# The prologue of a hybrid GLA and S5 block, put in another order

## The chip, the cores and the metric

The kernel runs on one core of one Trainium2 chip. The metric is the device time of one execution in microseconds (us), of which the median over several runs is taken; lower is better. The kernel before took 1011.63 us in the median of three runs (1009.40 to 1013.76).

## The reference, cut to what matters

One decoder block over 512 tokens, ahead of which 16 meta tokens are put. The model width is 1024. All numbers are float32.

```python
h = concatenate([meta, x])                       # 528 tokens x 1024
xn = rmsnorm(h, g_mix_pre)                       # x / sqrt(mean(x*x) + 1e-6) * gain
proj = xn @ w_in                                 # q, k, v, r, a_low, u, z_gla, z_ssm
log_a = log_sigmoid(a_low @ w_gate_up + b_gate) / 16
o = gla_chunked(q, k, v, log_a)                  # 4 heads, cumulative sums of log_a
...
# S5: 64 groups, 64 states, 16 channels each
lam = exp(a_re*dt) * (cos(a_im*dt), sin(a_im*dt))
bb = ((lam - 1) / a) * (b_re, b_im)              # (64, 64, 16), complex
y = Re(C scan(lam, bb u)) + d_skip * u
...
h = h + rmsnorm(mixed @ w_out, g_mix_post)       # gates, GLU and merge before it
h = h + rmsnorm(square(relu(hn @ w_ff1)) @ w_ff2, g_ffn_post)
```

## The kernel before

The program is written for a framework that takes the instructions in source order, gives each tile its memory, and sets the order in which each engine gets its instructions by a planner of its own when it is built. Source order is the priority; an instruction whose inputs the planner takes to be late can be passed by a later one. Each engine then runs its own list strictly in order, and so do the queues that issue loads (SP's, ScalarE's and GpSimd's). A tile in a memory pool that was opened after another was closed can lie on that one's memory, and its first writer then waits until the old tile is done with.

Every large product is done in three exact passes: a weight tile is split by `load_w` into a high part (ScalarE, line 101) and the remainder (VectorE, line 114), as are the activations (`transpose_tokens`, lines 101 and 138), and `mm3` (lines 121 to 123) adds high by high, high by low and low by high. `feat_tile` does this over the 8 tiles of the inner dimension, so a product of one weight tile of 128 columns with 264 tokens (half of the 528, `HALF`) is 24 matmuls. Raw weights and their two parts have three buffers each.

The part that is changed runs from the start to the first S5 block. In source order:

- **Constants.** A first activation on ScalarE at line 75 brings in its function table.
- **Input norm** (lines 166 to 206). Four tiles of 128 tokens are loaded by SP (line 178), the 16 meta tokens and the gain, broadcast to 128 partitions, by ScalarE's queue (lines 181 and 182). There are two groups: the meta tokens with tiles 0 and 1, then tiles 2 and 3. For each group come the sums of squares (line 195), the inverse root by an integer guess and three Newton steps on VectorE (`rsqrt`, 13 small instructions), the multiplication by root and gain (line 201) and the transposes on TensorE (line 135), with the split into `xh` and `xl`.
- **GLA gates** (lines 212 to 257). The 16 columns of `a_low` (48 matmuls of 16 columns), the product with `w_gate_up` (line 245), Abs, Exp and Ln on ScalarE (lines 247 to 250), and a scan on VectorE (line 255), written to DRAM as `bd`.
- **S5 parameters** (lines 260 to 444). Some 100 small instructions on VectorE give the powers of lambda (`Lr`, `Li`, `E8`). `c_re` and `c_im` come by GpSimd's queue (lines 411 and 412), and TensorE transposes them (line 417). `b_re` and `b_im` are loaded by SP in transposed order into `ra` and `rb`, two halves each (lines 423 to 426), in runs of 16 numbers; line 429 gives `rb` its sign. `BA` and `BB` follow from them (lines 434 to 440). Most of it depends on nothing but its own loads.
- **u products** (lines 454 to 462). Eight weight tiles, two halves of tokens each. ScalarE copies each half out of PSUM into `ut` (line 461), and GpSimd's queue writes that to DRAM as `ud`. The four PSUM banks named `mm` hold four halves. `ut` lies in pool `pgb`, which is opened after the gates' pool `pga` was closed.

After it four S5 blocks alternate with four GLA heads. An S5 block first forms its matrices on VectorE from `CA`, `CB`, `BA`, `BB` and the powers (lines 593 to 595), transposes one of them on TensorE (line 600) and later reads `ud`. A GLA head does four weight tiles of q, k and v (lines 470 to 520) and reads `bd`. Then come the gates' products, the merge, the output product and the MLP, which the change leaves alone.

Of the kernel before, what the change touches and what calls it, by code (L numbers as in the profile page):

```python
# [9 lines left out]
F32R = mybir.dt.float32r  # L10
# [6 lines left out]
P = 128  # L17
D = 1024
# [28 lines left out]
def hybrid_block(ctx: ExitStack, tc: tile.TileContext, io, out: bass.AP):  # L47
# [25 lines left out]
    warm = mk(cst, [P, 1], tag="warm")  # L73
    V.memset(warm, 1.0)
    S.activation(warm, warm, AF.Square)
# [27 lines left out]
    def load_w(src, ncol=256):  # L103
        """src: [K, ncol] in DRAM -> list of (hi, lo) [P, K/P, 128]."""
# [13 lines left out]
    def mm3(ps, whi, wlo, xhi, xlo, kt):  # L118
        """ps += w.T @ x by three exact passes; whi(k), xhi(k) give the k-th tiles."""
        for k in range(kt):  # L120
            PE.matmul(ps, whi(k), xhi(k), start=(k == 0), stop=False)  # L121
            PE.matmul(ps, whi(k), xlo(k), start=False, stop=False)  # L122
            PE.matmul(ps, wlo(k), xhi(k), start=False, stop=(k == kt - 1))  # L123

    def feat_tile(w, xh, xl, c0, c1, ps, m=P, kt=KT):
        hi, lo = w
        mm3(ps, lambda k: hi[:, k, :m], lambda k: lo[:, k, :m], lambda k: xh[:, k, c0:c1], lambda k: xl[:, k, c0:c1], kt)
# [12 lines left out]
    def cmul(pl, orr, oi, ar, ai, br, bi, shape, tag, eng=V, bufs=1):  # L140
        """o = a * b (complex), o apart from a and b"""
# [11 lines left out]
    def erot(E, n, m, pl):  # L153
        """E[:, :, :, n+1 : n+m+1] = E[..., n] * E[..., 1 : m+1], E [P, (re, im), g, c]"""
# [10 lines left out]
    # ================= input norm =================  # L165
# [5 lines left out]
    xl = mk(px, [P, KT, NT], F32R, tag="xl")  # L171
    sx = ExitStack()
    pxt = pool("pxt", stack=sx)
    gpre = mk(pxt, [P, D], tag="gpre")
    xts = []
    for t in range(TT):
        xt = mk(pxt, [P, D], tag="xt", bufs=5)
        nc.sync.dma_start(xt, io["x"][0, t * P : (t + 1) * P, :])
        xts.append((xt, P, NM + t * P))
    xm = mk(pxt, [P, D], tag="xt", bufs=5)  # L180
    nc.scalar.dma_start(xm[:NM], io["meta_tokens"])
    nc.scalar.dma_start(gpre, io["g_mix_pre"][0].partition_broadcast(P))
# [4 lines left out]
    xts = [(xm, NM, 0)] + xts  # L187
# [3 lines left out]
    for a, b in ((0, 3), (3, 5)):  # L191
        for i in range(a, b):
            xt, n, col = xts[i]
            sq = mk(pxt, [P, D], tag="xsq", bufs=2)
            S.activation(sq[:n], xt[:n], AF.Square, accum_out=ss[:n, i : i + 1])
        V.tensor_scalar(ss[:, a:b], ss[:, a:b], 1.0 / D, EPS, op0=ALU.mult, op1=ALU.add)
        rsqrt(rs[:, a:b], ss[:, a:b], pxt, f"xr{a}")
        for i in range(a, b):
            xt, n, col = xts[i]
            xn = mk(pxt, [P, D], tag="xn", bufs=2)  # L200
            V.scalar_tensor_tensor(xn[:n], xt[:n], rs[:n, i : i + 1], gpre[:n], op0=ALU.mult, op1=ALU.mult)
            transpose_tokens(xn[:n], n, xh, xl, col)
# [5 lines left out]
    w_in = io["w_in"][0]  # L208

    w_in = io["w_in"][0]  # L210

    # ================= GLA gates =================
    sg = ExitStack()
    pg = pool("pg", stack=sg)
# [15 lines left out]
    wgu = mk(pga, [16, 512], tag="wgu")  # L230
    nc.gpsimd.dma_start(wgu, io["w_gate_up"][0])
    wa = load_w(w_in[:, C_A : C_A + 16], 16)[0]
    alow = mk(pga, [16, NT], tag="alow")
    for i in range(2):
        ps = bank("mm")
        feat_tile(wa, xh, xl, i * HALF, (i + 1) * HALF, ps[:16, :HALF], m=16)
        S.copy(alow[:, i * HALF : (i + 1) * HALF], ps[:16, :HALF])
# [14 lines left out]
    for h in range(HEADS):  # L252
# [3 lines left out]
        nc.gpsimd.dma_start(bd[h], b2)  # L256
    sga.close()

    # ================= S5 parameters =================
# [8 lines left out]
    E8 = mk(p5, [P, 2, GRP, 9], tag="E8")  # L268
    V.tensor_reduce(i16, ident.rearrange("p (b h) -> p h b", h=HG), axis=mybir.AxisListType.X, op=ALU.add)
# [645 lines left out]
```

## Time and profile before

| what | value |
| --- | --- |
| median of three runs | 1011.63 us (1009.40 to 1013.76) |
| span of the profiled execution | 1011.4 us |
| TensorE busy, over the span | 954.4 us |
| VectorE busy | 573.3 us |
| ScalarE busy | 366.1 us |
| GpSimd busy | 61.3 us |

The profile gives no other time of that execution than its span, from the first to the last instruction. In its views a line names the start and the length in us, the engine, the line of the kernel, the operation and the tiles (out<-in). PE is TensorE, PEld its weight load, DVE is VectorE, ACT is ScalarE, POOL is GpSimd; SPq is the queue that issues SP's loads. A name of a tile without a number stands for all its buffers. The row of windows gives the busy time of each engine in a stretch, with the granted TensorE clock as a share of full speed. TensorE's matmuls overlap, so the time between their starts, not the duration of one, tells what a matmul costs.

### The profile page before, as it was taken

The numbers are of one execution on the slowest core, as the hardware profiler recorded it, in microseconds if no ns is written. First come the engines' busy times: TensorE is split into PE (matmuls) and PEld (weight loads), VectorE is DVE, ScalarE is ACT, GpSimd is POOL, SyncE is SP. The second block draws the span as 40 slices with busy tenths as digits, with TensorE's granted clock in tenths as the row PEclk, the third lists the DMA queues.
The fourth block names the chain that finished last, engine by engine and source line by source line (L and its number), as shares of the span: only waits on it lengthen the run. The fifth ranks groups of instructions, "written<-read, shape, count | busy, mean of one in ns | idle before, by whom it ended". The sixth has DMA issues, their size and how long they took to land.

```text
span 1011.4 us, 13388 instructions
## 1 busy us (share of the span) xinstructions
PE 954.4 (94%) x5120; PEld 806.1 (80%) x5120; DVE 573.3 (57%) x1098; ACT 366.1 (36%) x600; POOL 61.3 (6%) x128
## 2 busy tenths in 40 slices
PE   1779999999999999999999999899999999999996
PEld 1669978998878888888888877788888878888884
DVE  4979785968662787764544667633232343333327
ACT  3434344545443343333532432233222242332321
POOL 3110101010101101110000000000000000000000
PEclk9879999999999999999999999999999999999998
DMA  9534634252535564545854662042323254233202
GB/s 192 147 118 123 143 97 116 75 140 63 135 109 146 140 164 130 148 129 156 251 146 129 203 185 83 36 124 84 104 84 104 84 193 137 86 104 99 89 22 83
DMA packets 166080, 123.98 MB, mean 123 GB/s; under 512 B 33692, under 2 KB 148448, under 8 KB 166016
## 3 DMA queue, kind: packets, MB, share of 16 engines
q1 hardware_dynamic: 158944, 101.31, 36.2%
q0 software_dynamic: 6464, 19.65, 6.3%
q10 hardware_dynamic: 608, 2.16, 0.6%
q8 instruction: 40, 0.66, 0.3%
q14 instruction: 24, 0.20, 0.1%
HBM read 102.03 MB, written 16.81 MB: 117 GB/s over the span
## 4 chain that ended last, share of the span: by engine, by line
PE 78%; DVE 10%; issue 3%; DMA 3%; ACT 3%; SPq 2%; DVEq 0%; POOL 0%; ACTq 0%; POOLq 0%
PE mm L121 17%; PE mm L122 17%; PE mm L123 17%; PE mm L872 8%; PE sm L872 8%; PE sm L605 1%; PE sm L628 1%; PE sm L654 1%; PE sm L655 1%; SPq L424 1%; DVE wlo L114 1%; PE sm L600 1%; DMA wraw<-in_w_out_dram 1%; DMA vv<-vv 1%; DMA rb<-in_b_re_dram 1%
## 5 line engine op out<-in xcount | busy, mean ns | idle before, releaser
L114 DVE TENSOR_TENSOR wlo<-wraw,whi 128x1024 fp32r<-128x1024 f32 (+1 forms) x105 | 127.3, 1213 | 165.0 <-ACT whi L101 159.0
L101 ACT ACTIVATE whi<-wraw 128x1024 fp32r<-128x1024 f32 (+1 forms) x105 | 110.5, 1053 | 243.2 <-PE mm L122 217.0
L121 PE MATMUL mm<-xh,whi 128*128 128x264 f32 (+2 forms) x560 | 187.3, 335 | 6.3 <-ACT ut L461 4.5
L123 PE MATMUL mm<-xh,wlo 128*128 128x264 f32 (+2 forms) x560 | 186.4, 333 | 1.1 <-DVE wlo L114 1.1
L122 PE MATMUL mm<-xl,whi 128*128 128x264 f32 (+2 forms) x560 | 186.8, 334 | 0.0
L121 PEld LDWEIGHTS mm<-xh,whi 128*128 128x128 f32 (+1 forms) x560 | 104.7, 187 | 18.1 <-ACT ut L461 4.7
L123 PEld LDWEIGHTS mm<-xh,wlo 128*128 128x128 f32 (+1 forms) x560 | 104.8, 187 | 11.4 <-DVE wlo L114 1.3
L122 PEld LDWEIGHTS mm<-xl,whi 128*128 128x128 f32 (+1 forms) x560 | 104.8, 187 | 10.9 <-issue 1.0
L121 PE MATMUL mm<-hh,whi 128*128 128x512 f32 (+1 forms) x288 | 106.9, 372 | 0.0
L122 PE MATMUL mm<-hl,whi 128*128 128x512 f32 (+1 forms) x288 | 106.8, 371 | 0.0
L123 PE MATMUL mm<-hh,wlo 128*128 128x512 f32 (+1 forms) x288 | 106.6, 371 | 0.0
L863 DVE TENSOR_TENSOR fl<-f,fh 128x512 fp32r<-128x512 f32 x32 | 22.0, 692 | 84.6 <-ACT fh L101 84.6
L121 PEld LDWEIGHTS mm<-hh,whi 128*128 128x128 f32 x288 | 54.4, 190 | 10.4 <-ACT hh L101 0.2
L122 PEld LDWEIGHTS mm<-hl,whi 128*128 128x128 f32 x288 | 54.4, 189 | 10.3
L123 PEld LDWEIGHTS mm<-hh,wlo 128*128 128x128 f32 x288 | 54.3, 188 | 10.3
L101 ACT ACTIVATE fh<-f 128x512 fp32r<-128x512 f32 x32 | 20.0, 630 | 101.3 <-PE sm L872 101.3
L123 PE MATMUL mm<-gh,wlo 128*128 128x512 f32 x128 | 50.6, 395 | 0.0
L121 PE MATMUL mm<-gh,whi 128*128 128x512 f32 x128 | 50.6, 395 | 0.0
L122 PE MATMUL mm<-gl,whi 128*128 128x512 f32 x128 | 50.6, 395 | 0.0
L859 DVE TENSOR_TENSOR w2l<-wraw,w2h 128x1024 fp32r<-128x1024 f32 x32 | 39.1, 1225 | 7.2 <-ACT w2h L101 7.2
L872 PE MATMUL mm<-w2h,fh 128*128 128x512 f32 x128 | 40.0, 394 | 2.1 <-ACT fh L101 2.1
L872 PE MATMUL mm<-w2h,fl 128*128 128x512 f32 x128 | 40.3, 397 | 0.0
(378 smaller groups left out, 1655.7 us busy)
## 6 DMA issues: line engine op xcount, KB each, us to landing
wraw<-in_w_ff_dram SPq DMA_DIRECT2D x64, 512.0 KB, 4.0
wraw<-in_w_in_dram SPq DMA_DIRECT2D x48, 512.0 KB, 4.4
wraw<-in_w_glu_dram SPq DMA_DIRECT2D x16, 512.0 KB, 4.4
vv<-vv POOLq DMA_DIRECT2D x32, 130.0 KB, 3.3
xt<-in_x_dram SPq DMA_DIRECT2D x8, 512.0 KB, 5.6
M<-kpad SPq DMA_DIRECT2D x64, 64.0 KB, 3.4
wraw<-in_w_o_gla_dram SPq DMA_DIRECT2D x8, 512.0 KB, 4.4
wraw<-in_w_out_dram SPq DMA_DIRECT2D x8, 512.0 KB, 4.1
```

The source lines that it names most:

```text
L101: S.activation(dst, src, AF.Copy, scale=scale)
L114: V.tensor_sub(lo[:, :, :n], raw[:, :, :n], f32(hi)[:, :, :n])
L121: PE.matmul(ps, whi(k), xhi(k), start=(k == 0), stop=False)
L122: PE.matmul(ps, whi(k), xlo(k), start=False, stop=False)
L123: PE.matmul(ps, wlo(k), xhi(k), start=False, stop=(k == kt - 1))
L424: nc.sync.dma_start(ra[64:], bim)
L600: PE.transpose(ps[:, g * P : (g + 1) * P], MB[:, g0 + g].rearrange("p s h -> p (s h)"), ident)
L605: PE.matmul(ps[:, g * HG : (g + 1) * HG], M2[:, g, 0:8, :].rearrange("p l h -> p (l h)"), BA[:, blk * GB + g, :], start=True, stop=True)
L628: PE.matmul(pv[:, g], M1[:, g0 + g, :], U[:, g0 + g, :NST], start=True, stop=True)
L859: V.tensor_sub(lo, raw, f32(hi))
L863: V.tensor_sub(fl, f[:, k], f32(fh))
L872: PE.matmul(acc[t][n], a[:, ts_], b[:, n * 512 : (n + 1) * 512], start=st, stop=en)
```

## The change

The prologue is written in another order, and five things in it are done in another way.

- **Norm by tile.** Each token tile has its own root, but the meta tokens share that of tile 0. The root is a Sqrt activation on ScalarE, a reciprocal and one Newton step on VectorE. The table brought in at the start is the one with Sqrt. The gain comes as one row and is spread over 128 partitions by two products with a row of ones.
- **u first.** The first two weight tiles of u are loaded right behind x. The first token half of the first one is computed once the meta tokens and two tiles are there, that of the second behind the transposes of the third tile, and the two second halves follow behind the fourth. `ut` and `ud` move to pools that are opened before the norm.
- **Gates next, then the other six u tiles, then the S5 parameters.** The high and low parts of the 16 gate columns are put side by side in one weight tile of 32 columns, so 32 matmuls replace 48; `w_gate_up` is loaded twice, one copy under the other, and adds the two parts up. The gate columns' tile no longer uses the weights' buffers but pool `pga`, which lies on the norm's memory.
- **Held.** `tc.issue_after(i)` puts what is written inside it behind instruction i in the list of i's engine. The S5 parameters' work on VectorE stands behind the norm's last multiplication, and their loads on SP behind the last load of x.
- **b and c.** b is loaded as it lies (three loads, 64 partitions) and transposed by TensorE, 32 transposes in four PSUM tiles, with the sign given on the way out. c is loaded by SP's queue in place of GpSimd's.

```diff
-    S.activation(warm, warm, AF.Square)
+    S.activation(warm, warm, AF.Sqrt)
...
+    def root(y, ssum, pl, tag):
...
+        S.activation(a, ssum, AF.Sqrt, scale=1.0 / D, bias=epst[: shape[0]])
+        V.tensor_scalar(hm, ssum, 0.5 / D, 0.5 * EPS, op0=ALU.mult, op1=ALU.add)
+        V.reciprocal(y, a)
+        V.tensor_mul(a, y, y)
+        V.tensor_mul(a, a, hm)
+        V.tensor_scalar(a, a, -1.0, 1.5, op0=ALU.mult, op1=ALU.add)
+        return V.tensor_mul(y, y, a)
...
+    def u_half(w, ut, q):
+        ps = bank("mm")
+        last = feat_tile(w, xh, xl, q * HALF, (q + 1) * HALF, ps[:, :HALF])
+        S.copy(ut[:, :, q * 33 : (q + 1) * 33].rearrange("p s c -> p c s"), ps[:, :HALF].rearrange("p (c s) -> p c s", s=T8))
+        return last
...
+    def u_tile(shape=[P, T8, NCK]):
+        return mk(pg, shape, tag="ut", bufs=2)
...
+    nc.scalar.dma_start(grow, io["g_mix_pre"][0].rearrange("(o d) -> o d", o=1))
...
-    nc.scalar.dma_start(gpre, io["g_mix_pre"][0].partition_broadcast(P))
...
+    for i in range(2):
+        ps = bank()
+        PE.matmul(ps, one_row, grow[:, i * 512 : (i + 1) * 512], start=True, stop=True)
+        S.copy(gpre[:, i * 512 : (i + 1) * 512], ps)
...
-    for a, b in ((0, 3), (3, 5)):
-        for i in range(a, b):
...
-        V.tensor_scalar(ss[:, a:b], ss[:, a:b], 1.0 / D, EPS, op0=ALU.mult, op1=ALU.add)
-        rsqrt(rs[:, a:b], ss[:, a:b], pxt, f"xr{a}")
...
+    for i, (xt, n, col) in enumerate(xts):
+        sq = mk(pxt, [P, D], tag="xsq", bufs=2)
+        squared = S.activation(sq[:n], xt[:n], AF.Square, accum_out=ss[:n, i : i + 1])
+        if i == 0:
+            continue
+        a = 0 if i == 1 else i
+        root(rs[:, a : i + 1], ss[:, a : i + 1], pxt, f"xr{min(i, 2)}")
+        for xt, n, col in xts[a : i + 1]:
...
+            normed = V.scalar_tensor_tensor(xn[:n], xt[:n], rs[:n, j : j + 1], gpre[:n], op0=ALU.mult, op1=ALU.mult)
+            with ExitStack() as after:
+                if i > 2:
+                    after.enter_context(tc.issue_after(fed.ins))
+                transpose_tokens(xn[:n], n, xh, xl, col)
+        if i == 2:
+            with tc.issue_after(loaded.ins), tc.issue_after(squared.ins), tc.issue_after(normed.ins):
+                uw = load_w(w_in[:, C_U : C_U + 256])
+            uts = [u_tile() for _ in uw]
+        if i in (2, 3):
+            fed = u_half(uw[i - 2], uts[i - 2], 0)
+    for i in range(2):
+        u_half(uw[i], uts[i], 1)
+        u_out(i, uts[i])
...
-    wa = load_w(w_in[:, C_A : C_A + 16], 16)[0]
...
+    wraw = mk(pga, [P, KT, 16], tag="waraw")
+    nc.sync.dma_start(wraw, w_in[:, C_A : C_A + 16].rearrange("(k p) n -> p k n", p=P))
+    wa = mk(pga, [P, KT, 32], F32R, tag="wa")
...
+        for k in range(KT):
+            PE.matmul(ps[:32, :HALF], wa[:, k, :], xh[:, k, sl], start=(k == 0), stop=False, skip_group_check=True)
+            PE.matmul(ps[:16, :HALF], wa[:, k, :16], xl[:, k, sl], start=False, stop=(k == KT - 1), skip_group_check=True)
...
+    for c in range(256, D, 256):
+        for i, w in enumerate(load_w(w_in[:, C_U + c : C_U + c + 256])):
...
+    held = ExitStack()
+    held.enter_context(tc.issue_after(normed.ins))
+    held.enter_context(tc.issue_after(loaded.ins))
...
-        nc.gpsimd.dma_start(cnat[:, :, i, :], src)
-        nc.gpsimd.dma_start(cnatx[:, :, 1 - i, :], src)
+        nc.sync.dma_start(cnat[:, :, i, :], src)
+        nc.sync.dma_start(cnatx[:, :, 1 - i, :], src)
...
-    bre, bim = (io[n][0].rearrange("g n h -> n g h") for n in ("b_re", "b_im"))
-    nc.sync.dma_start(ra[:64], bre)
-    nc.sync.dma_start(ra[64:], bim)
-    nc.sync.dma_start(rb[:64], bim)
-    nc.sync.dma_start(rb[64:], bre)
+    bn = mk(q5, [N, 3, N, HG], tag="bn")
+    for i, name in enumerate(("b_re", "b_im", "b_re")):
+        nc.sync.dma_start(bn[:, i], io[name][0])
...
-    V.tensor_scalar_mul(rb, rb, nsgn)
+    for i, dst in enumerate((ra, rb)):
+        for h0 in range(0, HG, 8):
+            ps = bank()
+            pv = ps.rearrange("p (h g) -> p h g", h=8)
+            for h in range(8):
+                PE.transpose(pv[:, h], bn[:, i : i + 2, :, h0 + h], ident[:N, :N])
+            d = dst[:, :, h0 : h0 + 8].rearrange("p g h -> p h g")
...
-    for c in range(0, D, 256):
-        for i, w in enumerate(load_w(w_in[:, C_U + c : C_U + c + 256])):
-            blk = c // P + i
-            ut = mk(pgb, [P, T8, NCK], tag="ut", bufs=2)
...
```

More of the change, by code (lines that the diff above doesn't have):

```diff
@@ L74, in hybrid_block @@
     V.memset(warm, 1.0)
-    S.activation(warm, warm, AF.Square)
+    S.activation(warm, warm, AF.Sqrt)
+    epst = mk(cst, [P, 1], tag="epst")
+    V.memset(epst, EPS)
+    one_row = mk(cst, [1, P], tag="one_row")
+    V.memset(one_row, 1.0)
     ident = mk(cst, [P, P], tag="ident")
@@ L206, in hybrid_block @@
     sx.close()
[L208 to L214, printed above, removed]
     tri = mk(pg, [P, TT, P], I32, tag="tri")
@@ L256, in hybrid_block @@
         nc.gpsimd.dma_start(bd[h], b2)
+    for c in range(256, D, 256):
+        for i, w in enumerate(load_w(w_in[:, C_U + c : C_U + c + 256])):
+            ut = u_tile()
+            for q in range(2):
+                u_half(w, ut, q)
+            u_out(c // P + i, ut)
     sga.close()
```

56 lines of the change are left out of this document (31 added, 25 removed).

## The prediction

> **What bounds the kernel now.** I read the page first: its span, TensorE's row in the 40 slices and the chain of waits by engine.
>
> ```profile
> span 1011.4 us, 13388 instructions
> PE   1779999999999999999999999899999999999996
> PE 78%; DVE 10%; issue 3%; DMA 3%; ACT 3%; SPq 2%; DVEq 0%; POOL 0%; ACTq 0%; POOLq 0%
> ```
>
> TensorE (PE) is nearly full but for its first three slices, some 75 us, and the change touches only the work that lies there. So I cut that stretch into windows at the points where PE starts or stops. Columns: the stretch, its length, then busy us (instructions) of PE, of its weight loads, of VectorE (DVE), ScalarE (ACT) and GpSimd (POOL), the granted TensorE clock, the DMA share and GB/s.
>
> ```profile
> 0.00:20.40 20.40, 4.97 (x25) 4.29 (x25) 9.92 (x47) 9.45 (x18) 9.03 (x20) 1.00 0.99 214
> 20.40:30.10 9.70, 0.03 (x1) 0.00 (x0) 5.13 (x24) 0.60 (x1) 0.00 (x0) 0.69 1.01 168
> 30.10:35.00 4.90, 3.65 (x16) 3.27 (x16) 4.90 (x18) 4.04 (x6) 2.89 (x10) 0.56 0.77 200
> 35.00:41.50 6.50, 6.49 (x50) 4.75 (x50) 6.46 (x23) 0.95 (x3) 0.00 (x0) 1.00 0.06 13
> 41.50:57.40 15.90, 15.88 (x111) 14.28 (x110) 13.71 (x44) 10.58 (x15) 1.13 (x2) 1.00 0.39 112
> 57.40:61.90 4.50, 0.01 (x1) 0.01 (x1) 4.43 (x11) 1.65 (x3) 1.02 (x2) 0.98 0.55 167
> 61.90:64.00 2.10, 2.10 (x8) 1.81 (x8) 2.00 (x6) 1.43 (x3) 0.59 (x2) 0.50 0.87 323
> 64.00:66.70 2.70, 0.02 (x1) 0.00 (x1) 1.36 (x8) 0.00 (x0) 1.10 (x3) 0.50 1.00 283
> 66.70:72.00 5.30, 5.23 (x26) 4.71 (x27) 2.75 (x11) 2.68 (x5) 0.44 (x1) 0.50 0.27 96
> 72.00:106.00 34.00, 34.00 (x282) 34.00 (x281) 33.99 (x68) 14.28 (x23) 2.82 (x6) 1.00 0.40 113
> 125.00:1011.40 886.40, 863.01 (x4460) 720.64 (x4458) 474.14 (x827) 313.86 (x516) 38.95 (x77) 0.99 0.41 120
> ```
>
> To 72 us PE is busy 38.4 us (the nine rows) and idle 33.6. From 72 to 106 it has no gap, at 34.00/282 = 0.121 us a matmul, but DVE has none either: that is the second thing to watch. What the gaps wait for:
>
> ```profile
> PE mm L135 <- DVE xn L201: 15.7, 3, 9.7
> PE mm L121 <- ACT ut L461: 4.5, 1, 4.5
> PE sm L390 <- POOL nat L387: 2.7, 1, 2.7
> DVE rb L429 <- DMA rb<-in_b_re_dram: 4.4, 1, 4.4
> ```
>
> (us in all, times, longest). The 9.7 us from 20.4 wait for the norm of the last two token tiles. DVE stands in front of them with L429, the sign of `rb`, in the middle of the second square root, and that waits for a load. The queue that issues it:
>
> ```profile
> 3.78 3.17 SPq L423 DMA_DIRECT2D ra<-in_b_re_dram  x1
> 6.99 10.32 SPq L424 DMA_DIRECT2D ra<-in_b_im_dram  x1
> 19.95 2.54 SPq L426 DMA_DIRECT2D rb<-in_b_re_dram  x1
> 63.46 0.63 SPq L485 DMA_DIRECT2D b<-bd  x1
> 87.24 2.64 SPq L110 DMA_DIRECT2D wraw<-in_w_in_dram  x2
> ```
>
> One issue of b, a transposing load in runs of 16 numbers, holds SP for 10.3 us. So b delays the norm on DVE and the first u weights on SP. The 4.5 us at 57.4 are four full PSUM banks: ACT's copy into `ut` waits for memory of the gates.
>
> **The change part by part.** Durations:
>
> ```profile
> 2.54 0.20 ACT L75 ACTIVATE warm<-warm 128x1 f32<-128x1 f32 x1
> 8.62 1.04 ACT L195 ACTIVATE xsq<-xt 128x1024 f32<-128x1024 f32 x1
> 9.57 0.18 ACT L195 ACTIVATION_READ_ACCUMULATOR xsq<-xt 128x1 f32 x1
> 11.55 0.17 DVE L92 TENSOR_SCALAR xrs<-xss 128x3 int32<-128x3 int32 x1
> 13.96 0.15 DVE L98 TENSOR_TENSOR xrs<-xrs,xr_a 128x3 f32<-128x3 f32 x1
> 15.55 1.03 PE L135 MATMUL mm<-ident,xn 16*128 16x16 f32 x8 [5.82 <-DVE xn L201]
> 30.16 3.65 PE L135 MATMUL mm<-ident,xn 128*128 128x128 f32 x16 [9.73 <-DVE xn L201]
> 35.01 0.29 PE L121 MATMUL mm<-xh,whi 128*16 128x264 f32 x1 [1.21 <-DVE xl L138]
> 66.70 1.01 PE L390 MATMUL sm<-ident,nat 64*128 64x64 f32 x7 [2.68 <-POOL nat L387]
> L201 DVE SCALAR_TENSOR_TENSOR xn<-xt,xrs,gpre 128x1024 f32<-128x1024 f32 x4 | 5.0, 1270 | 0.0
> L138 DVE TENSOR_TENSOR xl<-mm,xh 128x512 fp32r<-128x512 f32 x8 | 5.3, 681 | 0.4 <-ACT xh L101 0.2
> L101 ACT ACTIVATE xh<-mm 128x512 fp32r<-128x512 f32 x8 | 4.6, 592 | 2.0 <-PE mm L135 2.0
> L114 DVE TENSOR_TENSOR wlo<-wraw,whi 128x1024 fp32r<-128x1024 f32 x5 | 6.0, 1209 | 0.0
> 70.39 0.74 DVE L419 TENSOR_SCALAR CA<-sm,sgn 128x512 f32<-128x512 f32 x1
> 105.94 0.87 PE sm L600 x8
> ```
>
> *Start of the products.* The first product was at 35.01. Now the first u half needs only the meta tokens and two tiles. The square of the first full tile is read out at 9.57 + 0.18 = 9.75. Two gain copies out of PSUM go ahead of it on ACT (2 x 0.59), then one Sqrt of a few columns, about the 0.20 of the one-column ACT row: 11.1. A small DVE step costs 0.2: the old root's 13 steps took 14.11 - 11.55 = 2.56. The new root has five behind the Sqrt, and I charge six, 1.2. Then on DVE two norms (2.54), a root (1.2) and a norm (1.27): 17.3. Behind it come eight transposes (1.8), the last ACT split (0.59) and DVE subtraction (0.68): **20.4**. Other subtractions and weight splits fit between. The loads of x compete with less, which is worth 0 to 2 us; I take 0 since the last gain rows must land too. Later than computed is possible by about 3, if DVE puts a weight split (1.2 each, two) before the last subtractions.
>
> *PE's idle time.* Up to 20.4, PE does 1.03 of small transposes and eight more pairs, 3.65: idle 15.7. Tiles 3 and 4 are transposed behind a u half each, and only the third half waits for a split: 0.59 + 0.68 = 1.3. The full banks at 57.4 go, since `ut` gets memory of its own. The 2.7 at 64.0 go if the six remaining u tiles cover POOL's copy; six tiles are 6 x 48 x 0.121 = 35 us of PE, ample. Idle 17.0 in place of 33.6: **-16.6**.
>
> *Added PE work.* The change adds 32 transposes of 64 rows for b. By the L390 row they cost 1.01/7 = 0.144 each, 4.6 us; by the 128-row ones 3.65/16 = 0.228, 7.3. I take 4.6, the same shape. The gate products fall from 48 to 32 at 0.121: -1.9. The gain's two broadcast products lie in the idle start.
>
> *Clock.* At 61.9 eight matmuls take 2.10 us, 0.26 each, at a granted 0.50, which lasts until about 72. The nine of before that ran so lose 9 x 0.14 = 1.3. The first half now comes behind sparse transposes, and may be slow: 24 x 0.14 = 3.4, bounds 0 and 6.8 (two halves). Net +2.1. The Trainium skill, page "TensorE: Matmul & The Clock Gate", part 1, says an idle window of about 3.4 us halves the clock, and about 3.4 us of work restores it. The 4.5 us gap agrees with it; the ten slow us after it, with a gap of 2.7 inside, are longer than its ramp. By the rule the first half would be slow for 3.4 us, 13 matmuls, which is 1.5 us less than charged.
>
> *DVE.* Four evictions of b (4 x 0.74, as c's at 70.39; 1.2 each, as for a weight split, if the permuted writes are slow) replace the sign of `rb` (0.75): +2.2. The S5 steps that sat inside the norm now stand behind its last multiplication, and no longer stall for 4.4. To 106 DVE was busy 84.7 us (its ten rows). From 11.1 it would do that, less 0.9 done earlier, plus 2.2 and some 3 of waits between norm steps: ready at 100, 6 us earlier than 106, while PE comes 12 earlier. Behind u, PE has the four products of the first GLA head, which need no S5 parameter: v 96 and k 48 matmuls at 0.121, and q 24 of 512 columns at about 0.24 (an estimate by the columns): 23 us. That is the cover, so I charge 0; without it, 6 us are given back.
>
> *Queues.* The c loads leave POOL and stand on SP with b's three plain loads, behind x and perhaps behind weights that wait for a buffer. ACT gets one more table load between Sqrt and Exp, covered by u work. POOL's gate masks still wait for the norm's memory.
>
> Sum: -16.6 + 4.6 - 1.9 + 2.1 = **-11.8**. The profiled span is 1011.4 and the median of the runs 1011.63, so what lies around the span is within 0.3: 1011.4 - 11.8 = 999.6. With the bounds (start 2 earlier or 3 later, b 2.7 more, clock -3.4 to +3.4, stalls 0 to 6) its own range is 993 to 1007.
>
> **Rivals.** *A, DVE becomes the bound.* If the GLA products aren't put in front, PE follows DVE: gain 6, **1005.5**. For it: DVE's 33.99 of 34.00. Against: PE worked on GLA weights around block 0 before, and DVE is busy only 474 of the 886 us after 125.
>
> *B, the loads set the start.* The DMA share is 0.99 to 20.4 us. With x and two weight tiles, 3 MB, at that row's 214 GB/s, 14 us, and the 7.7 us that an x tile took to land, products start at some 24 to 26: gain 7, **1004.5**. Against it: 214 was moved with b's short runs in between.
>
> ```profile
> xt<-in_x_dram SPq DMA_DIRECT2D x4, 512.0 KB, 7.7
> ra<-in_b_re_dram SPq DMA_DIRECT2D x1, 256.0 KB, 15.5
> ```
>
> *C, slower: c and b stuck on SP.* Before, SP issued nothing from 64.1 to 87.2, as weights waited for buffers. If c and b come behind such a wait, they land at about 95, with the 7.7 us of an x tile. From c's eviction at 70.4 to block 0's first transposes at 105.9 it took 35.5 us, so those come at 130, plus 5 for b's own transposes and evictions. at 135. PE would have reached that place at 106 - 12 = 94, and its cover ends at 94 + 23 = 117: 18 us idle against a gain of 11.8, so 1011.4 + 6.2, about **1018** with a slow clock after it. It decides once these loads land later than about 89, where idle and gain are equal. The Trainium skill, "DMA: Bandwidth & Descriptors", section "Issuing engines are not separate DMA queues", says another issuing engine saves only issue time; that gives the move no gain to set against C.
>
> *D, nothing gained.* The planner refills the freed time with other waits: **1011**.
>
> **How the numbers follow.** Forecast 0.60, A 0.18, B 0.10, C 0.06, D 0.06. Half a per cent, 5 us, is about what a measurement of this kernel can tell from no change. Faster means under 1006.5: nearly all of the forecast (0.59), 0.13 of A and 0.09 of B, 0.81 in all. Slower: 0.05, from C. The same: the rest, 0.14. The likeliest time is 999.5. The range 991 to 1007.5 takes the forecast's own, A and B, and below them two us for x landing early; it leaves out C, D and the edges.
>
> **What would show it.** Right: the first 264-column product at 18 to 23 us; no PE gap over 3 us between there and 72; no b load on SP over 1 to 2 us; S5 block 0's transposes near 100 with GLA products before them; later stages alike. Wrong: a PE gap at 90 to 120 behind DVE (A) or behind c and b on SP (C), a first product behind a weight load (B), or a slow clock for longer than the first two halves.

## The result, and the profile after

The changed kernel takes 1016.5 us in the median of 20 runs (1013.55 to 1022.69); the kernel before, run beside it, 1011.44 (20 runs, 1009.11 to 1018.16). The ratio is 1.0041, with a 95% interval of 1.0023 to 1.0060: 0.4% slower, where 12 us less were forecast.

First the page of the changed kernel: the span, TensorE's busy time and its row in the 40 slices, and the chain of waits by engine.

```profile
span 1011.8 us, 13443 instructions
PE 961.7 (95%) x5140; PEld 808.9 (80%) x5140; DVE 575.3 (57%) x1099; ACT 368.7 (36%) x607; POOL 57.9 (6%) x125
PE   5999879998999999999999999899999999999996
PE 74%; DVE 13%; issue 5%; DMA 4%; ACT 3%; POOL 0%; DVEq 0%; SPq 0%; POOLq 0%; ACTq 0%
```

The hole in the first three slices is nearly closed, as forecast, and yet the span is what it was. The spans differ by 0.4 us and the medians by 5.1, since the profiled execution is the fastest of the changed kernel's 20. What lies around a span is 1.7 to 1.8 us (1013.55 - 1011.8; another execution had 1016.17 and 1014.4), so the profiled execution of the kernel before, at 1011.4, took some 1013.1, above its median. The "within 0.3" of the prediction compared two different executions. The stretches below therefore show the direction, and nearly 5 us less than the whole loss.

Both kernels cut at the same points (columns as in the prediction), the kernel before first:

```profile
0.00:100.00 100.00, 66.37 (x465) 61.13 (x466) 78.66 (x236) 42.20 (x65) 18.49 (x43) 0.90 0.59 145
100.00:300.00 200.00, 196.25 (x1403) 175.93 (x1402) 148.50 (x290) 95.16 (x200) 19.32 (x39) 0.99 0.42 108
300.00:1011.40 711.40, 691.76 (x3256) 569.04 (x3254) 346.18 (x573) 228.75 (x335) 23.45 (x46) 0.99 0.42 123
```

and the changed one:

```profile
0.00:100.00 100.00, 87.42 (x636) 79.31 (x636) 74.47 (x228) 52.38 (x85) 16.18 (x41) 1.00 0.57 154
100.00:300.00 200.00, 181.03 (x1244) 158.95 (x1243) 153.71 (x301) 87.36 (x189) 17.75 (x37) 0.97 0.41 100
300.00:1011.80 711.80, 693.25 (x3264) 570.60 (x3262) 347.13 (x572) 228.97 (x336) 23.92 (x47) 0.99 0.42 123
```

To 100 us TensorE stands idle for 12.6 us instead of 33.6: 21.0 gained. From 100 to 300 it stands idle for 19.0 instead of 3.8: 15.2 given back. Its busy time over the whole span grows by 7.3 (961.7 - 954.4), and its idle time behind 300 us falls by 1.1 (19.6 to 18.6). Together: -21.0 + 15.2 + 7.3 - 1.1 = +0.4, the difference of the spans. Of the 21.0 and of the 7.3, 3.75 us are the gain's two broadcast products (four records), which fill idle time at the start and save nothing:

```profile
2.44 3.75 PE L225 MATMUL sm<-grow,one_row 1*128 1x512 f32 x4 [2.44 <-DMA grow<-in_g_mix_pre_dram]
```

So some 17.3 us of waiting went, and the rest of the added work, 3.5 us, is near the 2.7 (4.6 - 1.9) that was charged for b and the gates. Where the given-back time lies is seen when the changed kernel is cut at its own events: the first product (17.4), the first transposes of S5 block 0 (113.4), and the first product of that block that takes its scanned state into y (138.3).

```profile
0.00:17.40 17.40, 8.81 (x30) 5.42 (x30) 7.71 (x26) 12.54 (x25) 5.88 (x17) 1.00 0.92 248
17.40:60.00 42.60, 38.97 (x292) 35.60 (x292) 39.21 (x146) 24.06 (x34) 7.07 (x18) 1.00 0.58 143
60.00:80.00 20.00, 20.00 (x168) 19.79 (x167) 7.75 (x10) 9.98 (x16) 2.69 (x5) 1.00 0.66 198
80.00:113.40 33.40, 31.90 (x230) 29.54 (x231) 33.20 (x66) 8.97 (x15) 0.65 (x2) 1.00 0.27 71
113.40:138.30 24.90, 16.83 (x127) 16.30 (x125) 22.22 (x40) 3.14 (x7) 2.75 (x6) 0.91 0.37 76
```

In the kernel before the last of these stretches ran from 105.8 to 130.1:

```profile
105.80:130.10 24.30, 23.61 (x174) 22.00 (x172) 16.71 (x26) 6.96 (x14) 3.27 (x7) 1.00 0.63 141
```

Two things stand out. From 60 to 80 us VectorE works for 7.75 us of 20 while TensorE has no gap. And block 0's own chain, some 25 us long in both kernels, leaves TensorE idle for 8.1 us (24.90 - 16.83) where it left it idle for 0.7. The timeline of the changed kernel says what VectorE lacked: `nat`, the S5 parameters as 64 rows, was complete at 49.8 on GpSimd; its transposes ran at 79.3 on TensorE, and the copy into `prm` and all that needs it followed. Rows of GpSimd, TensorE and VectorE:

```profile
49.83 1.05 POOL L449 COPY nat<-nat 64x448 f32<-64x448 f32 x2 [11.45 <-DVE nat L445]
...
79.32 0.64 PE L452 MATMUL sm<-ident,nat 64*128 64x64 f32 x7
...
80.00 0.62 DVE L453 COPY prm<-sm 128x448 f32<-128x448 f32 x1 [1.82 <-PE sm L452]
```

TensorE was busy with the six remaining u tiles until then, and its list is run strictly in order. So the inputs of block 0 were ready 10 us later than before (`prm` was copied at 69.9 there), and the block came 7.6 us later, though u was done at 81.5 instead of 106.

### The profile page after: what moved, and what is told of

The parts are those of the page before. It is cut to its first block, busy times and chain, and to the rows that moved or that the text cites. A ratio compares the mean times of both kernels' runs of the same rounds, so it can differ in the third digit from the quotient of the medians.

```text
span 1011.8 us, 13443 instructions
## 1 busy us (share of the span) xinstructions
PE 961.7 (95%) x5140; PEld 808.9 (80%) x5140; DVE 575.3 (57%) x1099; ACT 368.7 (36%) x607; POOL 57.9 (6%) x125
## 4 chain that ended last, share of the span: by engine, by line
PE 74%; DVE 13%; issue 5%; DMA 4%; ACT 3%; POOL 0%; DVEq 0%; SPq 0%; POOLq 0%; ACTq 0%
PE mm L138 16%; PE mm L140 16%; PE mm L139 16%; PE mm L931 8%; PE sm L931 8%; DMA vv<-vv 2%; PE sm L664 1%; DVE wlo L131 1%; PE sm L687 1%; PE sm L713 1%; PE sm L714 1%; PE sm L621 1%; DMA wraw<-in_w_out_dram 1%; PE sm L622 1%; PE sm L659 1%
## 5 line engine op out<-in xcount | busy, mean ns | idle before, releaser
L131 DVE TENSOR_TENSOR wlo<-wraw,whi 128x1024 fp32r<-128x1024 f32 x104 | 127.2, 1223 | 167.0 <-ACT whi L118 161.1
L118 ACT ACTIVATE whi<-wraw 128x1024 fp32r<-128x1024 f32 x104 | 110.2, 1060 | 240.9 <-PE mm L139 222.6
L140 PE MATMUL mm<-xh,wlo 128*128 128x264 f32 (+1 forms) x544 | 180.5, 333 | 4.9 <-DVE wlo L131 4.9
L139 PE MATMUL mm<-xl,whi 128*128 128x264 f32 (+1 forms) x544 | 181.5, 334 | 1.6 <-DVE xl L156 1.6
L138 PE MATMUL mm<-xh,whi 128*128 128x264 f32 (+1 forms) x544 | 182.3, 336 | 0.7 <-ACT vt L534 0.4
L140 PEld LDWEIGHTS mm<-xh,wlo 128*128 128x128 f32 x544 | 103.0, 190 | 14.6 <-DVE wlo L131 5.2
L139 PEld LDWEIGHTS mm<-xl,whi 128*128 128x128 f32 x544 | 103.0, 189 | 11.9 <-DVE xl L156 2.1
L138 PEld LDWEIGHTS mm<-xh,whi 128*128 128x128 f32 x544 | 103.0, 189 | 11.8 <-ACT xh L118 0.8
L139 PE MATMUL mm<-hl,whi 128*128 128x512 f32 (+1 forms) x288 | 106.1, 369 | 0.0
```

Of the source, the lines that this page charges most:

```text
L118: S.activation(dst, src, AF.Copy, scale=scale)
L131: V.tensor_sub(lo[:, :, :n], raw[:, :, :n], f32(hi)[:, :, :n])
L140: last = PE.matmul(ps, wlo(k), xhi(k), start=False, stop=(k == kt - 1))
```

## The experiments

Four theories stood. *Theory 1*: the order in TensorE's list is the loss; the transposes that feed the S5 parameters (nat, then c and b) stand behind the six u tiles. *Theory 2*: the chain of S5 blocks and GLA heads sets the pace behind the prologue, so TensorE's work done earlier is worth nothing unless block 0 comes earlier too. *Theory 3*: transposing b on TensorE costs more than it saves. *Theory 4*: the planner's order is so sensitive that small edits move the time by some 5 us. In the summary the two columns of idle time are TensorE's, from the same windows as above; "block 0" is the start of its first transposes. Each ratio is against the kernel before, run beside it on the same chip. Its median was 1011.0 to 1012.8 us beside the different rows, so rows are compared by their ratios, not by their medians.

| kernel | median us | ratio (95%) | idle 0-100 | idle 100-300 | block 0 |
| --- | --- | --- | --- | --- | --- |
| before | 1011.44 | | 33.6 | 3.8 | 105.8 |
| after | 1016.50 | 1.0041 (1.0023-1.0060) | 12.6 | 19.0 | 113.4 |
| s5_before_u | 1010.10 | 0.9964 (0.9945-0.9983) | 18.3 | 5.8 | 100.4 |
| prm_before_u | 1011.79 | 0.9991 (0.9973-1.0009) | 13.3 | 15.2 | 110.2 |
| sqrt_table_alone | 1017.27 | 1.0049 (1.0030-1.0067) | 34.0 | 7.2 | 106.2 |
| b_on_pe_alone | 1017.25 | 1.0042 (1.0022-1.0062) | 34.0 | 2.5 | 114.3 |
| woven | 1008.67 | 0.9960 (0.9938-0.9981) | 14.3 | 9.7 | 98.9 |
| woven_b_by_dma | 1002.43 | 0.9907 (0.9884-0.9930) | 13.6 | 9.7 | 93.2 |
| held_alone | 1014.31 | 1.0031 (1.0010-1.0053) | 29.7 | 9.5 | 106.1 |
| act_copy_ahead_of_exp | 1013.76 | 1.0015 (0.9998-1.0032) | 33.5 | 5.0 | 105.3 |
| after_b_by_dma | 1012.23 | 1.0004 (0.9983-1.0025) | 16.7 | 17.0 | 113.4 |
| woven_b_by_dma_newton | 999.48 | 0.9880 (0.9852-0.9907) | 15.4 | 7.0 | 99.5 |
| woven_b_by_dma_unheld | 1002.53 | 0.9904 (0.9873-0.9936) | 14.9 | 9.7 | 92.7 |

**The order of u and the S5 parameters.** In `s5_before_u` the loop over the six later u tiles stands behind the S5 parameters; nothing else differs from the changed kernel.

```diff
     held.close()
     st5.close()
+    for c in range(256, D, 256):
+        for i, w in enumerate(load_w(w_in[:, C_U + c : C_U + c + 256])):
...
+            u_out(c // P + i, ut)
```

> The changed kernel with one move: the six later u tiles stand behind the S5 parameters in source order, as before the change. Theory 1 (priority: in the changed kernel the seven transposes of `nat`, ready at 51 us, wait on TensorE behind the six u tiles until 79.3, VectorE idles meanwhile, and S5 block 0's first transposes come at 113.4 in place of 105.9): here they run near 50 to 55, block 0's first transposes at 93 to 100, TensorE's idle time from 100 to 300 us falls from 19 us to under 8, and the time is 10 us or more below that of the changed kernel, about 1003 or less. Theory 2 (a fixed chain of the S5 blocks and GLA heads, their loads and VectorE, gives back any earlier start): block 0 comes earlier, but the idle time of 100 to 300 us stays near 19 and the time stays within 4 us of the changed kernel's. Theory 3 (the loss is in b and c): no change.

`prm` was copied at 57.9 instead of 80.0, block 0 came at 100.4, and the ratio fell from 1.0041 to 0.9964, with intervals apart. The windows of this kernel, cut at block 0 and at its y as above:

```profile
0.00:100.40 100.40, 82.13 (x532) 73.70 (x533) 85.46 (x250) 47.28 (x77) 15.77 (x41) 0.92 0.54 146
100.40:124.70 24.30, 24.30 (x180) 22.69 (x178) 16.51 (x26) 7.48 (x15) 3.29 (x7) 1.00 0.60 141
```

The block's own chain is now covered wholly (24.30 of 24.30, by u tiles that were left over). But the first row has idle time and a slow clock in it, and TensorE's timeline shows the new hole:

```profile
72.73 1.09 PE L488 MATMUL sm<-ident,bn 64*128 64x64 f32 x8
81.11 0.59 PE L140 MATMUL mm<-xh,wlo 128*128 128x264 f32 x1 [7.29 <-DVE wlo L131]
```

Now the low half of the u weights stands behind the S5 steps on VectorE. Theory 1 holds in its direction: by the ratios the move is worth 0.77%, some 8 us. It had set 10 us or more and 1003 or less, which did not come. The run also shows why neither end of the order is right: u first starves VectorE of transposes, and S5 first starves TensorE of split weights.

`prm_before_u` moves the same loop only behind the copy into `prm`, and leaves c, b, BA and BB behind it.

```diff
     V.tensor_scalar_mul(prm[:, E8I, :], prm[:, E8I, :], sgn)
+    for c in range(256, D, 256):
...
+            u_out(c // P + i, ut)
```

> The changed kernel with one part of the S5 parameters, down to the transposes of `nat` and the copy into `prm`, ahead of the six later u tiles; the powers, c and b stay behind them. Theory 1 in its narrow form (only the wait of `nat` on TensorE matters): VectorE's hole at 60 to 80 us closes in part and S5 block 0's first transposes come at about 105, since the transposes of c and b still stand behind u at 79; the time falls by some 5 to 8 us against the changed kernel. Theory 1 in its wide form (everything of S5 on TensorE that stands behind u counts): c and b hold block 0 at 108 or later and the time falls by under 4 us. Theory 2: no change in time.

`prm` came at 58.5, yet block 0 at 110.2, only 3.2 us earlier than in the changed kernel. VectorE's rows:

```profile
58.54 0.62 DVE L446 COPY prm<-sm 128x448 f32<-128x448 f32 x1
...
85.05 0.74 DVE L481 TENSOR_SCALAR CA<-sm,sgn 128x512 f32<-128x512 f32 x1
```

The transposes of c and b had taken the place of nat's behind the u tiles, and VectorE waited for those, as the wide form has it for block 0; the time fell by 0.50%, 5 us, where that form allowed under 4. So it is not one late instruction but a row of transposes. `woven` puts it between the u tiles: after the load of a pair of u weights comes a piece of the S5 parameters (to `prm`, the powers, c), then the pair's products.

```diff
+    uw = load_w(w_in[:, C_U + 256 : C_U + 512])
     sga.close()
...
+    for i, w in enumerate(uw):
...
+        u_out(256 // P + i, ut)
+    uw = load_w(w_in[:, C_U + 512 : C_U + 768])
     V.memset(Lr[:, 0, :], 1.0)
```

> The changed kernel with the six later u tiles woven into the S5 parameters in pairs: the first pair's weights are split ahead of the parameters and its products stand behind the transposes of `nat`, the second pair behind the work on c, the third behind the transposes of b. With the parameters first, block 0's first transposes came at 100.4 but TensorE stood 7.3 us for a u weight split behind them on VectorE, and ran slowly after it; with u first they came at 113.4. Theory 1 (both losses are queue order): here no TensorE gap over 3 us from 35 to 100, block 0's first transposes at 100 to 106, and a time 3 to 10 us below the one with the parameters first, 1000 to 1007. Theory 2 (the chain of S5 blocks and heads sets the pace, about 214 us from block 0's first transposes to those of block 4): block 4's come 214 to 223 us behind block 0's whatever TensorE did ahead, so the gain is that of block 0's start alone, 0 to 3 us against the parameters first.

Block 0 comes at 98.9, TensorE waits no longer than 1.1 us at a time between 35 and 100, and yet the ratio is 0.9960, like that of `s5_before_u`: the 3 to 10 us that theory 1 expected from closing the hole are not there, and theory 2's 0 to 3 fit. Against the changed kernel, some 8 us go with the order in both runs. Such a move also makes the planner set the later lists anew. Small edits moved the time by 3 to 5 us while block 0 stood still (`held_alone` and `sqrt_table_alone`, below); here it came 13 to 14.5 us earlier and the gain is larger, but how much of the 8 us belongs to the later lists is not shown.

**b on TensorE.** `b_on_pe_alone` puts the three plain loads of b, the 32 transposes and their evictions into the kernel before.

```diff
-    bre, bim = (io[n] ...
+    bn = mk(q5, [N, 3, N, HG], tag="bn")
...
```

> The kernel before with nothing but b loaded as it lies and transposed on TensorE, c still on GpSimd's queue. If b's transposing loads were what held the norm of the last tiles (9.7 us of TensorE idle) and the first weights: the first product comes 5 to 8 us earlier than 35.0, the added transposes cost 4.2 us, four slow evictions 4.6 of VectorE, and the time is 0 to 4 us below before. If the loads were hidden by something else, the first product stays at 33 or later and the time rises by 2 to 5 us.

The long issues of b were gone from SP, but the first product came at 37.36, later than the 35.01 of before. Rows of ScalarE, VectorE and TensorE:

```profile
22.31 1.06 ACT L101 ACTIVATE whi<-wraw 128x1024 fp32r<-128x1024 f32 x1 [8.26 <-DMA wraw<-in_w_in_dram]
...
23.51 0.35 DVE L138 TENSOR_TENSOR xl<-mm,xh 128x64 fp32r<-128x64 f32 x2 [6.74 <-ACT xh L101]
...
34.06 3.65 PE L135 MATMUL mm<-ident,xn 128*128 128x128 f32 x16 [6.92 <-DVE xn L201]
...
37.36 0.57 PE L121 MATMUL mm<-xh,whi 128*16 128x264 f32 x1
```

The planner set a weight split ahead of the split of x on ScalarE, that split waited until 22.3 for its weights, and the norm waited behind it: the wait for b was followed by another. With b's added work the time is 0.42% over that of before. Block 0 came at 114.3 instead of 105.8, so this is not the cost of the transposes alone. In the other direction, `after_b_by_dma` and `woven_b_by_dma` take the changed kernel and `woven`, and load b transposed as in the kernel before:

```diff
-    bn = mk(q5, [N, 3, N, HG], tag="bn")
...
+    bre, bim = (io[n] ...
```

> The changed kernel with one part undone: b is loaded transposed by DMA as in the kernel before, without the PE transposes and their evictions. Theory 1 (the order on TensorE's queue is the loss: nat's transposes stand behind the six u tiles): prm is still copied at about 80 us, block 0's first transposes still come after 110 us, TensorE still stands idle for 14 us or more between 100 and 300 us, and the time falls only by the TensorE work taken out, 4 to 5 us at most: 1011.5 to 1015. Theory 3 (the b transposes are the loss, by their 4.2 us on TensorE and by 3.9 us of evictions on DVE ahead of block 0): block 0's first transposes come 5 us or more earlier, idle of 100 to 300 us falls to 10 or less, and the time falls by 8 us or more, to 1005 to 1008.

> The woven kernel with b loaded in transposed order as before the change, behind the last load of x, in place of TensorE's 32 transposes. If these and their four evictions (2 x 0.95 and 2 x 1.04 us on VectorE) lie on the path: 3 to 6 us faster than the woven kernel. If the slow loads (10 us of issue on SP, some 15 us to land each) hold the u weights: a TensorE gap for a weight between 35 and 60 us, and 3 us slower or more.

In the changed kernel this moves the ratio from 1.0041 to 1.0004, some 4 us, and leaves block 0 at 113.4 and 17.0 us of idle time between 100 and 300 us: theory 1 foretold that, and theory 3 as the whole of the loss falls. In `woven` it moves it from 0.9960 to 0.9907, some 5 us. So b by TensorE costs about 4 to 5 us in two kernels; in the first of them the two intervals still just overlap. Its rows in the changed kernel, by line (TensorE 32 times, then VectorE's evictions):

```profile
L494 PE MATMUL sm<-ident,bn x32: 270/272/320, 81.8 to 94.3; 64*128 64x64 f32 x32
...
L499 DVE COPY ra<-sm x2: 1010/1011/1012, 91.6 to 92.5; 128x512 f32<-128x512 f32 x2
...
L497 DVE TENSOR_SCALAR rb<-sm,nsgn x2: 1039/1072/1105, 93.4 to 94.6; 128x512 f32<-128x512 f32 x2
```

(the columns are the shortest, middle and longest duration in ns, and the first and last start). Four evictions of 1.0 to 1.1 us are 4.2 us, on an engine that had 33.20 of the 33.40 us ahead of block 0 filled; and TensorE's busy time falls by 4.7 us from `woven` to `woven_b_by_dma` (964.9 to 960.2) and by 2.8 in the changed kernel (961.7 to 958.9). The load that this buys off is no burden any more once it is issued with x and the first weights landed: its four parts land in 4.9 to 6.9 us. SP's rows in `woven_b_by_dma`:

```profile
22.78 1.83 SPq L492 DMA_DIRECT2D ra<-in_b_re_dram  x1
...
28.94 0.61 SPq L493 DMA_DIRECT2D ra<-in_b_im_dram  x1
29.59 3.08 SPq L494 DMA_DIRECT2D rb<-in_b_im_dram  x1
...
38.79 0.72 SPq L495 DMA_DIRECT2D rb<-in_b_re_dram  x1
```

The issue of `in_b_im` into `ra` held SP for 10.3 us in the kernel before; it takes 0.6 here. `woven_b_by_dma` beats both kernels, by 0.93% against the one before.

**The hold.** `held_alone` adds to the kernel before only the rule that S5's work on VectorE stands behind the last normalized tile, and its loads on SP behind the last load of x.

```diff
+    held = ExitStack()
+    held.enter_context(tc.issue_after(normed.ins))
+    held.enter_context(tc.issue_after(loaded.ins))
     V.tensor_reduce(i16, ident ...
...
+    held.close()
     st5.close()
```

> The kernel before with nothing but the hold: S5's work on VectorE behind the norm's last multiplication, its loads on SP behind the last load of x. If the sign of `rb` and the S5 steps inside the norm were what delayed the products, the first product comes at 24 to 28 in place of 35.0. My prediction's reading then expects 5 to 9 us less time; theory 2 expects no more than block 0's start moves, which stays within 3 us of 105.8, and so a time within 3 us of before.

The first product came at 28.1 instead of 35.0, and the time got 0.31% longer: block 0 came at 106.1, as before (105.8), and TensorE's idle time went from 33.6 and 3.8 to 29.7 and 9.5. Seven microseconds were gained at the start and none at the end, and block 0 did not move, as theory 2 expects. Why the time rose by 3 us it does not explain. The other way round:

```diff
-    held = ExitStack()
-    held.enter_context(tc.issue_after(normed.ins))
-    held.enter_context(tc.issue_after(loaded.ins))
...
-    held.close()
```

> The kernel woven_b_by_dma without the hold that keeps the S5 parameters behind the norm's last tile and the last x load. If the early start comes from the hold: S5's loads and short DVE operations run ahead of or between the norm's tiles again, the first product comes at 22 us or later instead of 17.25, TensorE's idle time up to 35 us grows from 10.4 to 15 us or more, and the time is 1004 to 1010. Rival (the early start comes from the norm per tile and from u standing first; the S5 work fills gaps of DVE): the first product stays within 2 us of 17.25, block 0's first transposes come earlier than 93 us, and the time is 998 to 1002.

Without the hold the first product comes at 17.75, block 0 at 92.7, and the ratio is 0.9904 beside 0.9907: the rival was right (1002.53 us is at the edge of its 998 to 1002). In this kernel the early start needs no hold, and the hold is worth nothing that can be measured; that it comes from the norm by tile and from u standing first is what is left, and was not tried apart.

**The root by table.** `sqrt_table_alone` changes one word in the kernel before: the table brought in at line 75 is that of Sqrt.

```diff
-    S.activation(warm, warm, AF.Square)
+    S.activation(warm, warm, AF.Sqrt)
```

> The kernel before with nothing but its first activation made a Sqrt, so that ScalarE starts with that table. The profiled spans of before and after are 1011.4 and 1011.8, but the medians differ by 5 us. If the other first table costs time that the span doesn't hold, this kernel is 2 to 5 us slower than before with the same span. If not, one table load of 1.28 us is added ahead of Exp, off the path: within 1 us of before.

The kernel before computes no Sqrt, so all that this adds to ScalarE's work is one more table load ahead of Exp, in ScalarE's timeline:

```profile
47.75 1.28 ACT L249 ACT_TABLE_LOAD   x1
49.04 1.97 ACT L249 ACTIVATE ga<-ga 128x2112 f32<-128x2112 f32 x1
```

Yet the time rose by 0.49%, some 5 us, and the span with it (1011.4 to 1015.2), so neither half of the expectation held. TensorE's list was in another order afterwards (the transposes of nat and c seven places earlier, those of the second block thirteen), and its idle time between 100 and 300 us went from 3.8 to 7.2. To tell the delay from the order, `act_copy_ahead_of_exp` puts a copy of about that length, which nobody reads, in the place of the table load:

```diff
+    ga2 = mk(pga, [P, 1320], tag="ga2")
+    S.copy(ga2, ga.rearrange("p h t -> p (h t)")[:, :1320])
     S.activation(ga, ga, AF.Exp, scale=-1.0)
```

> The kernel before with a copy of 128 x 1320 numbers on ScalarE ahead of the gates' Exp, which nothing reads: about the 1.3 us of the added table load. The Sqrt table alone cost 4.9 us. If that was the delay of the gates, this costs 4 to 5 us too. If it was the other order that the planner then chose for the later heads (the second block's first transposes 13 rows earlier in TensorE's list, which here stand where they stood before), this costs under 1.5 us.

The ratio is 1.0015, and its interval takes in 1. The second block's transposes stand where they stood before, those of nat and c five places earlier. But the planner put the copy ahead of the last two Abs, so it delayed the gates by half as much only: Ln started at 50.54 in the kernel before, at 51.43 with the copy and at 52.32 with the table. So the delay may be a larger part of the 5 us than the 1.5 us of the copy; that the rest goes with the other order, as theory 4 has it, is likely and not shown. In the fastest version, the root of before was put back in:

```diff
-        S.activation(a, ssum, AF.Sqrt, scale=1.0 / D, bias=epst[: shape[0]])
...
+        ms = mk(pl, shape, tag=f"{tag}_m", bufs=2)
+        V.tensor_scalar(ms, ssum, 1.0 / D, EPS, op0=ALU.mult, op1=ALU.add)
+        return rsqrt(y, ms, pl, tag)
```

> The kernel woven_b_by_dma with the norm's root computed as before (an integer estimate and three Newton steps on DVE, still per token tile), and the first table load that of Square. If the table root helps: each of the four roots is some 7 short DVE operations longer, the first product comes 0.5 to 2 us later than 17.25 us, and the time is 1002.5 to 1005. Rival (the extra table load of 1.28 us ahead of Exp, or the order that goes with it, costs more than the root saves, as with the table alone in the kernel before): the first product comes up to 2 us later all the same, but the gates come earlier, and the time is 997 to 1001.

The first product comes 1.6 us later (18.89), and the ratio is 0.9880 beside 0.9907. The intervals overlap, so whether it is faster stays open; no gain of the table root shows. The rival had expected the gates earlier, which did not come (Ln at 52.0 and 52.1). And block 0 came at 99.5 instead of 93.2 without costing time: its start alone does not set the end either, so theory 2 holds in part only.

## Why the prediction was wrong

*The start, and TensorE's early idle time: right.* The first product was forecast for 20.4 and came at 17.38: the roots of two tiles run between each other on VectorE, so the first multiplication started at 11.13 where I had 12.3, and the second root cost nothing on the path. TensorE's idle time to 72 us was forecast at 17.0 and is 12.2; but the gain's products had been left in the idle time there, and with their 3.75 us the like figure is 16.0. Its longest wait between there and 72 us was 1.8, within the 3 that I had set.

*The clock: mis-sized.* I charged 2.1 us, since the first half might run slow. From 18.52 us on the products' starts are 0.12 us apart, so it did not. The transposes ahead of it ran slowly, though the window to 17.40 prints a clock of 1.00: sixteen took 3.82 us, as the sixteen of the kernel before did at a granted 0.56 (3.65), and eight took 1.07 a little later.

```profile
13.65 3.82 PE L153 MATMUL mm<-ident,xn 128*128 128x128 f32 x16 [0.17 <-DVE xn L240]
23.38 1.07 PE L153 MATMUL mm<-ident,xn 128*128 128x128 f32 x8 [1.78 <-DVE xr_a L104]
```

The charge per slow product was too high as well: in the kernel before their starts are 0.22 us apart (62.28, 62.50, 62.72), so each loses 0.10, not 0.14. The slow stretch came later, at 113 to 138 us (0.91) and on to 144 (0.50), behind waits of 3.8 and 4.4 us.

*b: nearly right on TensorE, wrong on VectorE.* 4.6 us were charged on TensorE; the whole part costs 4 to 5 us in the experiments. The evictions were taken at 0.74 us each and took 1.0 to 1.1.

*The step that failed* is the one on VectorE with its cover: "ready at 100, 6 us earlier than 106", and "That is the cover, so I charge 0". It failed in two places.

First, I let VectorE go on working from 11.1 us without asking for its inputs. I had counted nat's transposes, which could no longer leave TensorE idle, as a gain ("The 2.7 at 64.0 go if the six remaining u tiles cover POOL's copy"), and called six tiles of cover ample. For TensorE they were; for VectorE, which waits for these transposes, they were a delay of 28 us, from 50.9 (49.83 + 1.05) to 79.3. VectorE lost 12.25 us between 60 and 80 (20 - 7.75), and block 0 came at 113.4, not at 100. My estimate of 100 with these 12 us added would have been 112. The runs that move the order bear this out: block 0 came at 100.4 and 98.9 there.

Second, the 23 us of products of the first GLA head were there, but they can cover only once. TensorE's groups from 79.3 to 113.4 in the changed kernel, while it waited for block 0:

```profile
L138 PE MATMUL mm<-xh,whi 128*128 128x264 f32 x53 | 15.4, 292 | 0.4 <-ACT vt L534 0.4
...
L140 PE MATMUL mm<-xh,wlo 128*128 128x512 f32 x8 | 3.3, 409 | 1.1 <-DVE wlo L131 1.1
```

and from 113.4 to 138.3, in block 0's own chain:

```profile
L140 PE MATMUL mm<-xh,wlo 128*128 128x264 f32 x28 | 8.7, 316 | 3.8 <-DVE wlo L131 3.8
```

In the kernel before that chain had 44 products of this line as cover, of 264 and 512 columns:

```profile
L123 PE MATMUL mm<-xh,wlo 128*128 128x264 f32 (+1 forms) x44 | 13.5, 306 | 0.0
```

All 24 products of 512 columns, and some of 264, now stand ahead of the block instead of inside it. That is not the whole: the wait of 3.8 us in the row is for a weight split that VectorE began at 125.19 only, 12 us after ScalarE had the high part ready (112.03 + 1.06), and VectorE is filled for 22.22 us of this stretch, against 16.71 in the kernel before. So a part of the cover was there and not yet split; no run tells the two apart. TensorE's waits between 95 and 300 us show what it ran into instead (us in all, times, longest), the changed kernel first:

```profile
PE sm L714 <- DVE vv L706: 5.3, 3, 4.4
PE mm L140 <- DVE wlo L131: 4.9, 2, 3.8
PE sm L609 <- ACT kmeta L591: 4.5, 3, 2.0
```

and the kernel before:

```profile
PE sm L576 <- ACT on L571: 1.3, 3, 0.6
PE mm L123 <- DVE wlo L114: 1.1, 1, 1.1
```

So the 21.0 us gained by 100 us (17.3 without the gain's products) were not a gain in time but work done ahead, and the chain behind it, which came later, took 15.2 of them back. I had charged 0 for what is given back, with a bound of 6. The range was too narrow by its own terms, too: its bounds added up reach from 994 to 1014.7, not 993 to 1007.

*The rivals.* D (nothing gained, other waits take the freed time) was the nearest, with 0.06; it named no place, and the place could be read from source order: `nat` is written behind the u loop. C's 1018 lies nearer in number, by luck, for what it describes did not happen. A saw VectorE as the bound, but for its own length, and did not see its wait. B and C did not happen: b's plain loads were issued from 22.9 to 26.1 us and landed in 7.2 to 7.5.

*What the runs say of the parts.* With the S5 parameters woven into u and b left to the DMA, the rest of the change gains 0.93%, or 1.2% with the old root: 9 to 12 us, the size that I had forecast for the whole. That is luck in part: without the 4.6 us for b the forecast's terms give 16.4, so some of the freed time is given back even there (idle 9.7 and 7.0 us between 100 and 300 instead of 3.8). The mechanism of the forecast was there; the change as written spends it on the order of TensorE's list and on b.

## What to carry to other kernels

When work is moved ahead on an engine that runs its list in order, ask of every small instruction that now stands behind it who waits for its result on another engine: seven transposes that cost TensorE 0.64 us cost VectorE 12. Cover is spent once: before charging nothing for a wait, look up what the covering work covers now. And do not take idle time that goes at the start for a gain: in `held_alone` seven microseconds went at the start, and the end came no earlier. The next fixed point of the dependency chain (here block 0's first transposes) tells more, but not all: in `woven_b_by_dma_newton` it came 6 us later than in `woven_b_by_dma`, and the time was no longer.

## What the runs showed of the hardware

How long an issue holds SP differs by more than ten times for the same load. `in_b_im` into `ra`, transposing, held SP for 10.32 us when it was issued at 7.0 us, right behind four x tiles, a weight tile and another b load; at 28.9 us into `woven_b_by_dma`, right behind two other loads (at 22.78 and 24.73), it held SP for 0.61. The busy share of the DMA engines alone doesn't tell it: it was 1.15 in the windows of both the 10.32 us issue and the 0.72 us one at 38.8. What sets it was not tried.

After one gap the clock stayed low for some 6 us of work. In `s5_before_u` the gap of 7.29 us was followed by this stretch without another one; the matmuls' starts are 0.22 us apart up to 87.0 and 0.12 from there:

```profile
81.10:87.00 5.90, 5.89 (x27) 5.89 (x27) 5.90 (x7) 0.60 (x1) 0.00 (x0) 0.50 0.73 193
87.00:91.80 4.80, 4.80 (x41) 4.80 (x41) 4.80 (x9) 1.65 (x3) 0.54 (x1) 0.99 0.63 146
```

TensorE worked for 5.9 us before the full clock was granted again. In the changed kernel, too, the 5.9 us from 138.3 to 144.2, behind a wait of 4.4, ran at a granted 0.50. The Trainium skill, page "TensorE: Matmul & The Clock Gate", part 1, gives about 3.4 us of sustained work for it, in windows that run on freely, whatever the kernel does. The 5.9 us of the row are more than one such window and less than two.

A one-word edit that adds a table load of 1.28 us to ScalarE moved the end by 5 us, and a copy of the same length, which delayed the gates by half as much, by 1.5 with an interval that takes in 0. With a planner that sets the order anew for each build, an edit's own cost and the order that comes with it have to be measured apart; here they were so in part only.
